# A PSUM tile of one bank for each Strassen product of the second FFN, its written-out order laid out anew, and the load of its first weights moved by one step

## The chip, the cores and the metric

The kernel runs on one core of a Trainium2 chip. The metric is the device time of one execution in microseconds, lower is better. The engines are called as the profile calls them: PE (matmul), DVE (vector), ACT (scalar), POOL, and SP, which here only issues loads. Each engine carries out its own list of instructions in order and waits at an instruction until the semaphores that it names have been reached.

## The reference

Two layers of a transformer over 512 positions with 1024 channels, in fp32. Layer 0 has a Fourier and Hyena mixer, layer 1 an attention with low-rank queries and keys (MLA); after each comes a convolutional FFN with 2816 inner columns. The change touches the second FFN and the projection ahead of it:

```python
D_MODEL = 1024
SEQ = 512
D_FF = 2816

def _dwconv3(x, w, b):
    xp = jnp.pad(x, ((0, 0), (1, 1), (0, 0)))
    return xp[:, :-2] * w[0] + xp[:, 1:-1] * w[1] + xp[:, 2:] * w[2] + b

def _conv_ffn(h, w_up, conv_w, conv_b, w_down):
    gate, val = jnp.split(h @ w_up, 2, axis=-1)
    return (jax.nn.silu(_dwconv3(gate, conv_w, conv_b)) * val) @ w_down
```

## The kernel before

Everything is kept transposed: channels on the 128 partitions, the 512 positions along the free axis. Each large product is made of three matmuls, hi·hi, hi·lo and lo·hi (`mm3`, L195 to L198), where ACT makes the rounded part hi of an operand (L171) and DVE the rest lo (L176). Weights come from HBM through the pool `W`, which has three buffers each of the raw weights `wr`, of `wh` and of `wl`; SP issues those loads in order (L184), so a load whose buffer isn't free yet holds back all loads behind it.

The output projection of the attention (`res_proj`, L1147) goes through the eight output blocks m twice, for the first 256 positions and then for the last 256. The second pass takes m in the order 5, 6, 7, (0, 1), 2, 3, 4, as j = 0 to 7, where 0 and 1 are already done. Each m adds its product to the residual stream `xr` (L1188), and the sums of squares of `xr` feed the norm whose output, hi and lo, are the tiles `hh` and `hl` that the FFN reads. `whook` is called after each m; at the step after m=3 it issues the two loads of the FFN's first weights (block 0 of `w_up`, twice 512 KB).

The second FFN (`ffn_blocks`, L1790) has 22 blocks f of 128 inner columns, each a gate half and a value half. Blocks 0 and 1 are computed whole (step `U`). Blocks 2 to 21 are computed by the Strassen-Winograd scheme, where the 1024 channels and the 512 positions are split in two: seven products P1 to P7 of 12 matmuls of 128x256, in the order P1 P2 P5 P6 P7 P4 P3, instead of eight. The additions between them:

- `S1`, `S2`, `S4` make sums of weight blocks. `S1` is POOL's four adding DMAs, `S2` (L1876) and `S4` (L1879) are DVE additions that need the block's raw weights, loaded by `Rv`. `Ha`, `La`, `Hb`, `Lb` make hi and lo of the sums, `Hv`, `Lv`, `Hg`, `Lg` those of the plain weights.
- P1, then P6 and then P4 are written to columns 0 to 255 of a PSUM tile `m`; P2 and then P7 to columns 512 to 767 of the same tile. P5 and P3 go to a tile `ms` of another tag. PSUM is 16 KB for each partition, in 8 banks of 512 fp32; `mm` tiles have 1024 columns, two banks, and there are three of them.
- `K1` (ACT, L1926) copies P1 to `t`. `C1` (DVE, L1929, fv<-t,mm) adds P2. `Ua` (t<-t,mm) adds P6, `Ub` (t<-t,mm) adds P7, `Xv` (fv<-t,ms) P5, `C2` (fg<-t,ms, L1932) and `C4` (fg<-t,mm) make the gate's two halves, `C3` (fv<-fv,ms) the value's.
- `Ca` (ACT, L1962), `Cb`, `Cc` (DVE, L1966, L1970), `Si` (ACT, L1973), `Ml` (DVE, L1976), `Ah`, `Al` are the convolution, SiLU, product with the value, and hi and lo of the result.

The blocks form groups (0 to 4, 5 to 9, 10 to 13, 14 to 17, 18 to 21). After a group its share of the product with `w_down` is made: for each of 8 output blocks a load `Rd`, `Hd` and `Ld` for hi and lo, a product `D` of 15 or 12 matmuls of 128x512 in an `mm` tile, and `X` (DVE, L2029), which adds it to `xr`. The steps D of group g stand between the P steps of later blocks.

The order of all these steps, on PE, DVE, ACT, SP and POOL, is the text `UP_ORDER` (L86): the steps are issued one by one from it, each to its engine, and nothing is reordered. A matmul that writes a tile waits for the readers of what was in it, and a reader waits for the last matmul that wrote it. Both go by the tile as a whole: the pool is opened so (`reuse_waits = "tile"`), and the tile `m` of a block is one tile, though its two halves are in different banks. What waits for what follows from the place in the list. Where C1 stands behind P6, it waits for P6, whose half it doesn't read; where it stands ahead, P6 waits for C1. P7 waits for C1 in both cases, Ua stands behind P7 and waits for it, though it reads P6, and P4 waits for Ub, though it writes where only Ua read.

Of the kernel before, what the change touches and what calls it, by code (L numbers as in the profile page):

```python
# [9 lines left out]
F32 = mybir.dt.float32  # L10
# [8 lines left out]
P = 128  # L19
# [67 lines left out]
S1.2 Rv2 Rv3 Rg2 S1.3 Hv2 S2.2 T1 Ha2 U1 Lv2 Ca0 Th1 La2 Hg2 Tl1 T3 S4.2 Th3 T2 Rv4 Hb2 Cb0 Th2 Tl3 Lb2 Tl2 S1.4 Cc0 P1.2 Ca1 T4 Si0 P2.2 Lg2 Th4 Ml0  # L87
K1.2 S2.3 P5.2 Ah0 C1.2 Hv3 Tl4 P6.2 Lv3 P7.2 Ha3 Ua2 S4.3 Xv2 P1.3 Rg3 Ub2 La3 P4.2 Rv5 K1.3 C2.2 Cb1 P3.2 S2.4 Hg3 Cc1 Lg3 P2.3 Si1 C3.2 Hb3 Ml1 P5.3
C4.2 Hv4 Lb3 Ah1 P6.3 C1.3 S1.5 Lv4 P7.3 Ha4 Ua3 S4.4 P1.4 Xv3 Rg4 Ub3 La4 P4.3 Rv6 K1.4 C2.3 Al0 P3.3 Al1 Ca2 C4.3 Hg4 Cb2 Ca3 P2.4 Lg4 Hb4 Cc2 P5.4
C3.3 Si2 Lb4 Hv5 P6.4 C1.4 S1.6 Lv5 P7.4 Ua4 S2.5 Xv4 P1.5 Ha5 Ub4 Ml2 C2.4 P4.4 Ah2 La5 K1.5 P3.4 S4.5 Cb3 Rg5 C4.4 P2.5 Cc3 Hb5 C3.4 Rv7 Al2 Si3 P5.5  # L90
Lb5 Hv6 Hg5 P6.5 C1.5 S1.7 Ca4 Lv6 P7.5 Lg5 Ua5 S2.6 P1.6 Ub5 Ha6 Xv5 C2.5 P4.5 Ml3 K1.6 La6 Ah3 P3.5 S4.6 Cb4 Rg6 P2.6 Hb6 C3.5 Cc4 S2.7 Rd0.0 P5.6
Si4 Lb6 Hv7 P6.6 Hg6 C1.6 S1.8 Lv7 P7.6 Ha7 Lg6 Ua6 C4.5 P1.7 Ub6 Xv6 C2.6 P4.6 La7 K1.7 Ml4 P3.6 S4.7 Ah4 Al3 Rg7 P2.7 Al4 Hb7 C4.6 C3.6 Rd0.1 Ca5
P5.7 Lb7 Hd0.0 Hg7 C1.7 P6.7 S1.9 Ca6 Ld0.0 Lg7 Rd0.2 P7.7 Cb5 Hd0.1 Rv8 Ua7 Cc5 D0.0 Ub7 Si5 Xv7 C2.7 Ld0.1 S2.8 Rd0.3 Ml5 P4.7 S4.8 Ah5 X0.0 Cb6 P3.7
C4.7 Cc6 D0.1 Al5 Si6 C3.7 Hd0.2 Ml6 Hv8 Ld0.2 Ca7 Lv8 Rg8 Ah6 D0.2 Cb7 Ha8 Rd0.4 X0.1 La8 Hg8 Lg8 Cc7 P1.8 Hb8 X0.2 Al6 Si7 P2.8 Lb8 K1.8 Ml7 P5.8
# [8 lines left out]
Rd1.7 Hd1.5 Ua13 Xv13 Ld1.5 D1.4 Ub13 Rv14 C2.13 S2.14 P4.13 X1.4 S4.14 P3.13 C4.13 Ca13 D1.5 Cb13 Hd1.6 C3.13 Hd1.7 Ld1.6 Ld1.7 Rv15 Cc13 Si13 D1.6
Rg14 X1.5 Hv14 Ml13 Lv14 Ah13 Hg14 S2.15 Rv16 Lg14 D1.7 Ha14 X1.6 S4.15 La14 Al13 P1.14 Hb14 X1.7 P2.14 Lb14 K1.14 S1.16 P5.14 Hv15 C1.14 P6.14 Lv15
Rg15 P7.14 Ha15 Ua14 Xv14 Rd2.0 P1.15 La15 Ub14 P4.14 C2.14 K1.15 P3.14 Hg15 C4.14 Ca14 S2.16 P2.15 Lg15 Hb15 C3.14 S4.16 P5.15 Lb15 Hv16 C1.15 P6.15
S1.17 Lv16 P7.15 Cb14 Rg16 Ha16 Ua15 Cc14 P1.16 Xv15 Rd2.1 Si14 Ub15 La16 P4.15 K1.16 C2.15 Ml14 P3.15 Hg16 C4.15 Ah14 Lg16 Ca15 P2.16 Al14 Hb16 C3.15
# [17 lines left out]
class Builder:  # L124
# [30 lines left out]
    def mm(self):  # L155
        return self.t(self.ps, [P, 1024], F32, "mm", 3)
# [62 lines left out]
    def setup(self):  # L219
# [3 lines left out]
        self.ps = self.pool("psA", space=PSUM)  # L223
        self.sm = self.pool("sm", bufs=2)
# [1532 lines left out]
    def layer1(self, x, hh, hl, steps, aw):  # L1757
# [12 lines left out]
        self.ps = self.pool("psA", space=PSUM)  # L1770
        half = [[(0, 256)], [(256, 256)]]
# [21 lines left out]
    def ffn_blocks(self, x, hh, hl, quarter, first, steps):  # L1793
# [121 lines left out]
        def P7(f):  # L1915
            prod(k_["m", f][:, 512:768], k_["wb", f], 512, tf(3))
# [24 lines left out]
        def Ub(f):  # L1941
            plus(k_["t", f][:, 2, :], k_["t", f][:, 1, :], k_["m", f][:, 512:768])
# [331 lines left out]
```

## Time and profile before

| | us |
|---|---|
| three runs | 1656.69, 1652.11, 1655.27 (median 1655.27) |
| profiled execution, whole time | 1651.85 |
| its span (first to last instruction) | 1650.0 |
| PE busy in the span | 1576.6 (96%) |
| DVE, ACT, POOL busy | 1174.0 (71%), 670.9 (41%), 166.3 (10%) |
| granted PE clock over the span | 0.988 of full |

The profiled execution is 3.42 us faster than the median of the runs and its time is 1.85 us longer than its span. The rows of the profile used below are of four kinds: waits grouped by the waiting instruction and what released it; busy time in stretches of time (windows), with the granted PE clock; single instructions in order of time (timeline), with the idle time before each in brackets and what ended it; and DMA issues with their time to landing.

### The profile page before, as it was taken

Reading aid. Unit: us, or ns where it says so; the run is one execution under the profiler, and the core shown is the slowest. Engines: PE = TensorE matmul, PEld = TensorE weight load, DVE = VectorE, ACT = ScalarE, POOL = GpSimd, SP = SyncE. Lnnn points to the kernel's source line nnn. Section 1 sums busy time; section 2 is a strip of 40 time slices with the busy share of each in tenths; the row PEclk is TensorE's granted clock in tenths of the full one; section 3 lists DMA queues with packets and bytes.
Section 4 is the critical chain, followed back from the end, with each engine's and each line's share of the span. In section 5 each row is a group of like instructions: output and inputs, shape, how many; then the busy total and the mean of one; then the engine's idle time right before and its main releaser. Section 6 shows DMA issues by size and latency. Waiting matters only on the chain. (4 is left out here: it accounts for less than half of the span.)

```text
span 1650.0 us, 22867 instructions
## 1 busy us (share of the span) xinstructions
PE 1576.6 (96%) x8968; PEld 1319.7 (80%) x8968; DVE 1174.0 (71%) x1963; ACT 670.9 (41%) x980; POOL 166.3 (10%) x245
## 2 busy tenths in 40 slices
PE   7999999999999999999999999999998899999899
PEld 5787888888888888888888877666568888888787
DVE  6779869877885356553454666899977887767784
ACT  4441234433223112221122337898855544434342
POOL 0021133000000000000000001122220121102100
PEclk9999998999999999999999999999999999999999
DMA  9336502633443245432442310000062464545433
GB/s 359 107 103 229 154 29 79 204 102 128 154 154 125 64 130 163 145 115 64 129 149 77 106 33 1 16 8 13 4 213 84 108 157 127 146 128 141 135 97 109
DMA packets 68122, 189.25 MB, mean 115 GB/s; under 512 B 7979, under 2 KB 15341, under 8 KB 66989
## 3 DMA queue, kind: packets, MB, share of 16 engines
q1 hardware_dynamic: 59053, 166.79, 31.3%
q0 software_dynamic: 8960, 20.98, 6.1%
q8 instruction: 71, 1.16, 0.3%
q14 instruction: 38, 0.31, 0.1%
HBM read 181.97 MB, written 5.77 MB: 114 GB/s over the span
## 5 line engine op out<-in xcount | busy, mean ns | idle before, releaser
L196 PE MATMUL mm<-hh,wh 128*128 128x512 f32 (+2 forms) x1192 | 395.2, 333 | 2.7 <-ACT hh L349 1.4
L197 PE MATMUL mm<-hl,wh 128*128 128x512 f32 (+2 forms) x1192 | 394.4, 331 | 2.5 <-DVE hl L358 2.3
L198 PE MATMUL mm<-hh,wl 128*128 128x512 f32 (+2 forms) x1192 | 393.2, 330 | 0.3 <-DVE wl L176 0.3
L171 ACT ACTIVATE wh<-wr 128x1024 fp32r<-128x1024 f32 (+3 forms) x187 | 177.7, 957 | 425.5 <-PE mm L197 391.5
L176 DVE TENSOR_TENSOR wl<-wr,wh 128x1024 fp32r<-128x1024 f32 (+3 forms) x187 | 207.2, 1113 | 119.7 <-ACT wh L171 119.2
L196 PEld LDWEIGHTS mm<-hh,wh 128*128 128x128 f32 x1192 | 224.7, 189 | 31.9 <-issue 2.9
L197 PEld LDWEIGHTS mm<-hl,wh 128*128 128x128 f32 x1192 | 224.5, 188 | 27.5 <-DVE hl L358 3.3
L198 PEld LDWEIGHTS mm<-hh,wl 128*128 128x128 f32 x1192 | 224.6, 188 | 22.5 <-DVE wl L176 0.9
L281 DVE SCALAR_TENSOR_TENSOR junk<-wr,sb 128x1024 bf16<-128x1024 f32 x128 | 156.2, 1221 | 50.5 <-DMA wr<-wmodT 50.5
L196 PE MATMUL mm<-ah,wh 128*128 128x512 f32 (+1 forms) x480 | 172.0, 358 | 3.8 <-ACT wh L171 3.8
L198 PE MATMUL mm<-ah,wl 128*128 128x512 f32 (+1 forms) x480 | 172.8, 360 | 2.1 <-DVE wl L176 2.1
L197 PE MATMUL mm<-al,wh 128*128 128x512 f32 (+1 forms) x480 | 171.9, 358 | 0.0
L1188 DVE SCALAR_TENSOR_TENSOR xr<-mm,mod,xr 128x512 f32<-128x512 f32 (+1 forms) x76 | 43.7, 594 | 90.6 <-PE mm L198 89.0
L196 PEld LDWEIGHTS mm<-ah,wh 128*128 128x128 f32 x480 | 90.2, 188 | 18.9 <-ACT wh L171 6.0
L198 PEld LDWEIGHTS mm<-ah,wl 128*128 128x128 f32 x480 | 90.2, 188 | 18.1 <-DVE wl L176 4.7
L197 PEld LDWEIGHTS mm<-al,wh 128*128 128x128 f32 x480 | 90.3, 188 | 13.3
L1656 PE MATMUL pv<-S,V 128*128 128x512 f32 x192 | 93.8, 597 | 2.5 <-ACT S L1635 2.5
L1610 ACT ACTIVATE S<-s,rks 128x512 f32<-128x512 f32 x96 | 62.6, 686 | 12.4 <-PE pv L1656 8.5
L411 POOL MEMSET kvh<- 128x2 f32 x1 | 0.1, 99 | 633.4 <-PE mm L197 633.4
L1656 PEld LDWEIGHTS pv<-S,V 128*128 128x128 f32 x192 | 34.4, 190 | 34.8 <-issue 29.4
L1628 POOL PARTITION_ALL_REDUCE mx<-mx x16 | 44.8, 2803 | 164.6 <-DVE mx L1625 164.6
L196 PE MATMUL mm<-th,wh 128*128 128x256 f32 x160 | 47.0, 294 | 13.7 <-DVE fv L1929 12.4
(404 smaller groups left out, 3220.4 us busy)
## 6 DMA issues: line engine op xcount, KB each, us to landing
wr<-wmodT SPq DMA_DIRECT2D x80, 512.0 KB, 3.5
wr<-w_up SPq DMA_DIRECT2D x68, 512.0 KB, 3.5
sum<-w_up POOLq DMA_DIRECT2D x80, 256.0 KB, 4.2
wm<-wmod0a SPq DMA_DIRECT2D x8, 1024.0 KB, 10.4
wr<-w_in SPq DMA_DIRECT2D x16, 512.0 KB, 3.9
wr<-w_dn SPq DMA_DIRECT2D x16, 512.0 KB, 3.5
wr<-w_out SPq DMA_DIRECT2D x13, 512.0 KB, 3.7
wr<-w_o SPq DMA_DIRECT2D x11, 512.0 KB, 3.8
```

What stands on the lines that cost most here:

```text
L171: self.nc.scalar.activation(dst, src, AF.Copy)
L176: (eng or self.nc.vector).tensor_tensor(dst, src, hi.bitcast(F32), op=ALU.subtract)
L196: mmul(out, wh, xh, start=start, stop=False)
L197: mmul(out, wh, xl, start=False, stop=False)
L198: mmul(out, wl, xh, start=False, stop=stop)
L281: nc.vector.scalar_tensor_tensor(junk, raw, 1.0, self.sb[:, j, :], op0=ALU.mult, op1=ALU.mult, accum_out=acc)
L411: self.nc.gpsimd.memset(t[:, 512:514].bitcast(F32), 0.0)
L1188: nc.vector.scalar_tensor_tensor(x[m][:, a2:b2], ps[:, a2:b2], mod[:, 8 * sec + m, c : c + 1], x[m][:, a2:b2], op0=ALU.mult, op1=ALU.add)
L1610: nc.scalar.activation(c.S[a][j // 3][:, j % 3, :], c.ps[a, j], AF.Copy, scale=c.r[:, g : g + 1])
L1628: nc.gpsimd.partition_all_reduce(c.m[a][:, 1, :], c.m[a][:, 0, :], P, bass.bass_isa.ReduceOp.max)
L1656: nc.tensor.matmul(c.P[a], V[:, j, o : o + 128], c.S[a][j // 3][:, j % 3, :], start=j == 0, stop=j == 5)
```

## The change

Three parts change, and the number of instructions on each engine stays the same.

1. In the second FFN and the projection ahead of it the `mm` tile has 512 columns, one bank, and there are six (`self.mmw`; 1024 and three elsewhere). P1, P6 and P4 of a block use one tile, P2 and P7 another of their own; blocks 0 and 1 use a tile for the gate and one for the value.
2. `UP_ORDER` is laid out anew. The sequences of PE (181 steps), SP (80 steps) and POOL (20 steps) in it stay word for word; those of DVE (436 steps) and ACT (210) change.
3. The two loads of block 0's weights are issued at the last step of the projection (j = 7) and not at the one before.

Of `UP_ORDER` the diff shows two pieces, the stretch of block 12 and that of block 3:

```diff
-Si11 Ld1.1 D1.0 Ub12 Rv13 Ml11 C2.12 Ah11 Al11 S2.13 P4.12 X1.0 S4.13 P3.12 C4.12 Ca12 D1.1 Cb12 Hd1.2 C3.12 Hd1.3 Ld1.2 Ld1.3 Rd1.4 Cc12 Rg13 Si12
+Rd1.3 D1.0 Ld1.1 Ub12 Rv13 Ml11 C2.12 Ah11 Al11 P4.12 X1.0 P3.12 S2.13 C4.12 S4.13 D1.1 Ca12 C3.12 Hd1.2 Cb12 Hd1.3 Ld1.2 Ld1.3 Rd1.4 Cc12 D1.2 Rg13
-C4.2 Hv4 Lb3 Ah1 P6.3 C1.3 S1.5 Lv4 P7.3 Ha4 Ua3 S4.4 P1.4 Xv3 Rg4 Ub3 La4 P4.3 Rv6 K1.4 C2.3 Al0 P3.3 Al1 Ca2 C4.3 Hg4 Cb2 Ca3 P2.4 Lg4 Hb4 Cc2 P5.4
+P5.3 Si1 Lb3 Hv4 P6.3 C1.3 S1.5 Lv4 P7.3 Ha4 Ua3 Rg4 Ml1 P1.4 Xv3 Ah1 Ub3 La4 Rv6 P4.3 K1.4 C2.3 Al0 P3.3 Al1 Ca2 C4.3 Hg4 Cb2 P2.4 Ca3 Lg4 Hb4 Cc2
...
     def mm(self):
-        return self.t(self.ps, [P, 1024], F32, "mm", 3)
+        return self.t(self.ps, [P, self.mmw], F32, "mm", 3072 // self.mmw)
...
+        self.mmw = 1024
...
         self.ps = self.pool("psA", space=PSUM)
+        self.mmw = 512
...
         def whook(stage, j, m):
             hook(stage, j, m)
-            if stage and j == 6:
+            if stage and j == 7:
                 first.extend(self.wload(I["w_up"][1, 0, q]) for q in range(2))
...
         def P1(f):
-            m = k_["m", f] = self.mm()
-            prod(m[:, 0:256], k_["wv", f], 0, part(0, 0))
+            k_["m", f] = self.mm()
+            prod(k_["m", f][:, 0:256], k_["wv", f], 0, part(0, 0))
 
         def P2(f):
-            prod(k_["m", f][:, 512:768], k_["wv", f], 512, part(1, 0))
+            k_["n", f] = self.mm()
+            prod(k_["n", f][:, 0:256], k_["wv", f], 512, part(1, 0))
...
         def P7(f):
-            prod(k_["m", f][:, 512:768], k_["wb", f], 512, tf(3))
+            prod(k_["n", f][:, 0:256], k_["wb", f], 512, tf(3))
...
         def C1(f):
             k_["v", f] = self.t(tm, [P, T], F32, "fv", 3)
-            plus(k_["v", f][:, 0:256], k_["t", f][:, 0, :], k_["m", f][:, 512:768])
+            plus(k_["v", f][:, 0:256], k_["t", f][:, 0, :], k_["n", f][:, 0:256])
...
         def Ub(f):
-            plus(k_["t", f][:, 2, :], k_["t", f][:, 1, :], k_["m", f][:, 512:768])
+            plus(k_["t", f][:, 2, :], k_["t", f][:, 1, :], k_["n", f][:, 0:256])
...
         def U_(f, halves, ks):
             if ("m", f) not in k_:
-                k_["m", f] = self.mm()
+                k_["m", f], k_["n", f] = self.mm(), self.mm()
```

The instructions of DVE in block 3, from the lo part of the weight sum for P7 (Lb3) to Ub3; the last number of a name is the tile's own, so equal numbers are one tile. Before:

```order
L1932 SCALAR_TENSOR_TENSOR fg_11425<-t_11335,mm_11303 128x256
L176 TENSOR_TENSOR wl_11461<-sum_11208,wh_11460 128x1024
L1929 TENSOR_TENSOR fv_11497<-t_11423,mm_11392 128x256
L176 TENSOR_TENSOR wl_11479<-wr_11284,wh_11478 128x1024
L1929 TENSOR_TENSOR t_11423<-t_11423,mm_11392 128x256
L1879 TENSOR_TENSOR sum_11297<-sum_11296,wr_11284 128x512
L1929 TENSOR_TENSOR fv_11497<-t_11423,ms_11464 128x256
L1929 TENSOR_TENSOR t_11423<-t_11423,mm_11392 128x256
```

After (the lines of the code are three further down):

```order
L176 TENSOR_TENSOR wl_11464<-sum_11209,wh_11463 128x1024
L1932 TENSOR_TENSOR fv_11498<-t_11424,mm_11446 128x256
L176 TENSOR_TENSOR wl_11484<-wr_11286,wh_11483 128x1024
L1932 TENSOR_TENSOR t_11424<-t_11424,mm_11395 128x256
L1979 TENSOR_TENSOR fq_11319<-fq_11319,mm_11223 128x512
L1932 TENSOR_TENSOR fv_11498<-t_11424,ms_11468 128x256
L1932 TENSOR_TENSOR t_11424<-t_11424,mm_11446 128x256
```

C1 (fv<-t,mm), Ua and Ub (t<-t,mm) read one tile before, 11392; now C1 and Ub read 11446, that of P2 and P7, and Ua reads 11395, that of P1 and P6. S4 of block 4 (sum) has left the stretch for an earlier place, and Ml of block 1 (L1976 before, L1979 now) has come in.

DVE where block 12 ends and the weights of block 13 are summed. Before: Al11, S2.13 (sum<-sum,wr), X1.0 (xr), S4.13 (sum), C4.12 (fg), Cb12 (fq), C3.12 (fv).

```order
L176 TENSOR_TENSOR al_12960<-fq_12853,ah_12959 128x512
L1876 TENSOR_TENSOR sum_12769<-sum_12769,wr_12954 128x512
L2029 SCALAR_TENSOR_TENSOR xr_1889_10471<-mm_12937,mod_5_74,xr_1889_10471 128x512
L1879 TENSOR_TENSOR sum_12770<-sum_12769,wr_12954 128x512
L1932 SCALAR_TENSOR_TENSOR fg_12957<-t_12828,mm_12796 128x256
L1966 SCALAR_TENSOR_TENSOR fq_12991<-fg_12957,pcol_67,fq_12991 128x511
L1929 TENSOR_TENSOR fv_12902<-fv_12902,ms_12873 128x256
```

After:

```order
L176 TENSOR_TENSOR al_12973<-fq_12878,ah_12972 128x512
L2032 SCALAR_TENSOR_TENSOR xr_1889_10471<-mm_12949,mod_5_74,xr_1889_10471 128x512
L1878 TENSOR_TENSOR sum_12781<-sum_12781,wr_12967 128x512
L1935 SCALAR_TENSOR_TENSOR fg_12970<-t_12842,mm_12808 128x256
L1881 TENSOR_TENSOR sum_12782<-sum_12781,wr_12967 128x512
L1932 TENSOR_TENSOR fv_12915<-fv_12915,ms_12886 128x256
L1969 SCALAR_TENSOR_TENSOR fq_13020<-fg_12970,pcol_67,fq_13020 128x511
```

X1.0 now stands ahead of S2.13, the instruction that waits for the load Rv13, and C4.12 ahead of S4.13.

SP's loads at the end of the projection: `w_o` of m=2, m=3 and m=4 and the first two of `w_up` are block 0's. Before:

```order
L184 DMA wr_10863<-w_o 128x1024
L184 DMA wr_10906<-w_o 128x1024
L184 DMA wr_10945<-w_up 128x1024
L184 DMA wr_10951<-w_up 128x1024
L184 DMA wr_10957<-w_o 128x1024
L184 DMA wr_11020<-w_up 128x1024
```

After:

```order
L184 DMA wr_10863<-w_o 128x1024
L184 DMA wr_10906<-w_o 128x1024
L184 DMA wr_10945<-w_o 128x1024
L184 DMA wr_10984<-w_up 128x1024
L184 DMA wr_10990<-w_up 128x1024
L184 DMA wr_11020<-w_up 128x1024
```

The load for m=4 has moved ahead of block 0's two.

More of the change, by code (lines that the diff above doesn't have):

```diff
@@ L91 @@
[L91 to L94, printed above, removed]
@@ L103 @@
[L103 to L106, printed above, removed]
@@ L1957, in gate @@
         def gate(f):
-            return k_["m", f][:, 0:512] if f < UP_WHOLE else k_["g", f]
+            return k_["m", f] if f < UP_WHOLE else k_["g", f]
         def Ca(f):
```

56 lines of the change are left out of this document (32 added, 24 removed).

## The prediction

> **What bounds the kernel now.** I read the busy times first, then PE's waits, then single stretches.
>
> ```profile
> PE 1576.6 (96%) x8968; PEld 1319.7 (80%) x8968; DVE 1174.0 (71%) x1963; ACT 670.9 (41%) x980; POOL 166.3 (10%) x245
> ```
>
> PE is the bound over the whole, so a change that leaves its 8968 matmuls as they are can only win PE's idle time. What PE waited for in the blocks of Strassen products (1290 to 1650 us; total us, times, longest):
>
> ```profile
> PE mm L196 <- DVE fv L1929: 12.4, 12, 3.4
> PE mm L196 <- DVE t L1929: 5.2, 9, 1.0
> PE mm L196 <- ACT wh L171: 5.0, 7, 1.3
> PE mm L198 <- DVE wl L176: 2.5, 6, 0.5
> ```
>
> The first two rows are 21 waits for C1 and for Ua or Ub, 17.6 us; the other two are 13 waits of D for hi and lo of its weights, 7.5 us. Each costs more than its idle time:
>
> ```profile
> 1310.08 0.28 PE L196 MATMUL mm<-th,wh 128*128 128x256 f32 x1
> 1311.69 0.42 DVE L1929 TENSOR_TENSOR fv<-t,mm 128x256 f32<-128x256 f32 x1 [1.09 <-PE mm L198]
> 1312.26 0.36 PE L196 MATMUL mm<-th,wh 128*128 128x256 f32 x1 [0.61 <-DVE fv L1929]
> 1312.45 0.28 PE L197 MATMUL mm<-quarter,wh 128*128 128x256 f32 x1
> 1312.57 0.28 PE L198 MATMUL mm<-th,wl 128*128 128x256 f32 x1
> 1313.94 0.42 DVE L1929 TENSOR_TENSOR t<-t,mm 128x256 f32<-128x256 f32 x1 [0.70 <-PE mm L198]
> ```
>
> This is block 3. Matmuls follow each other at 0.12 us, but each row lasts 0.28, so an idle time that counts from the end of a row leaves out 0.16 us: a wait costs its idle time plus 0.16. P6 starts at 1310.08; C1 waits until P6 has ended, though it reads P2's half; P7 waits for C1 and starts at 1312.26; and Ua, which needs only P6, waits for P7. The product that a step reads was long done; the wait is for the tile.
>
> **The tile of its own.** C1 now depends on P2 and K1, Ua on P6, Ub on P7; P6 waits for K1 alone, P7 for C1, P4 for Ua. In block 3 C1 comes after Lb3 while P6 runs, and P7 finds it done. So all 21 waits should go, (12.4 + 5.2) + 21 × 0.16 = 21.0 us, less two remainders.
>
> The first is the longest, 3.4 us, P6 of block 2:
>
> ```profile
> 1295.76 1.28 ACT L1973 ACT_TABLE_LOAD   x1 [1.51 <-DVE fq L1970]
> 1298.54 0.35 ACT L1926 COPY t<-mm 128x256 f32<-128x256 f32 x1
> 1299.26 1.22 DVE L176 TENSOR_TENSOR quarter<-quarter,th 128x1024 fp32r<-128x1024 f32 x1
> 1299.39 0.39 PE L196 MATMUL mm<-th,wh 128*128 128x256 f32 x1 [3.40 <-DVE fv L1929]
> ```
>
> K1 stands on ACT behind the table load for SiLU and ends at 1298.89. P6 needs it, so it can start only some 0.45 us earlier, and P7 behind it needs the lo part that DVE makes right after C1 (1299.26, 1.22 long). I take 0.3 as won here: 3.2 us of the 3.56 stay.
>
> The second is DVE's own load in blocks 2 to 6, where no D gives PE other work:
>
> ```profile
> 1300.00:1350.00 50.00, 46.25 (x382) 44.77 (x381) 43.73 (x73) 23.84 (x33) 11.58 (x16) 1.00 0.60 145
> ```
>
> 382 matmuls at 0.117 are 44.7 us of these 50. DVE (43.73 in the third column) overlaps its rows by 0.08 (in a fence below a row of 0.69 at 1450.90 is followed at 1451.51), so it occupies 43.73 − 73 × 0.08 = 37.9 us of some 45: 84%. It fits, but it does so in order, with little slack in any one block: I leave 0.8 us. The term is 21.0 − 3.2 − 0.8 = **17.0 us**; its bounds are 11 (DVE late in every second wait) and 20.6.
>
> **The waits of D.** The chain shows best where block 12 ends:
>
> ```profile
> 1450.90 0.69 DVE L1876 TENSOR_TENSOR sum<-sum,wr 128x512 f32<-128x512 f32 x1 [2.51 <-DMA wr<-w_up]
> 1451.51 0.74 DVE L2029 SCALAR_TENSOR_TENSOR xr<-mm,mod,xr 128x512 f32<-128x512 f32 x1
> 1452.17 0.68 DVE L1879 TENSOR_TENSOR sum<-sum,wr 128x512 f32<-128x512 f32 x1
> 1452.77 0.41 DVE L1932 SCALAR_TENSOR_TENSOR fg<-t,mm 128x256 f32<-128x256 f32 x1
> 1453.22 0.81 ACT L1962 ACTIVATE fq<-fg,pcol 128x512 f32<-128x512 f32 x1 [5.56 <-DVE fg L1932]
> 1453.94 1.35 ACT L171 ACTIVATE wh<-wr 128x640 fp32r<-128x640 f32 x2
> 1454.71 0.50 PE L196 MATMUL mm<-ah,wh 128*128 128x512 f32 x1 [0.63 <-ACT wh L171]
> 1455.93 0.50 PE L198 MATMUL mm<-ah,wl 128*128 128x512 f32 x1 [0.49 <-DVE wl L176]
> 1446.09 0.33 SPq L184 DMA_DIRECT2D wr<-w_up  x1
> ```
>
> S2 of block 13 idles DVE for 2.51 us for its load, issued at 1446.09 when Ld1.1 had freed a buffer. X, S4 and C4 are queued behind it; ACT's Ca waits 5.56 us for C4, Hd1.2 is queued behind Ca, and D1.2 gets its weights late. Two things change. X goes ahead of S2 and S4 behind C4: C4 starts (1451.51 − 1450.90) = 0.6 us after S2 and not 1.87, 1.26 us won. And C1 no longer holds DVE until P6 ends:
>
> ```profile
> 1442.19 0.42 DVE L1929 TENSOR_TENSOR fv<-t,mm 128x256 f32<-128x256 f32 x1 [1.74 <-PE mm L198]
> 1444.45 0.42 DVE L1929 TENSOR_TENSOR t<-t,mm 128x256 f32<-128x256 f32 x1 [0.44 <-PE mm L198]
> ```
>
> C1 goes 1.74 us earlier, Ua up to (1444.45 − 1442.19) = 2.26 earlier, the two Ld with them, and so the buffer is free and the load lands some 2 us sooner. Together that is over 3 us ahead against 0.63 + 0.49 wanted, and the other groups have the same order. The 13 waits are 7.5 + 13 × 0.16 = 9.6 us; I leave 0.6 for the first of a group, where three loads are in line: **9.0 us**, bounds 3 and 9.6. What is late next is the sums: S2 and S4 stand later in DVE's list. In block 13 La ends at 1463.24 and P5, which needs it, starts at 1465.29:
>
> ```profile
> 1462.02 1.22 DVE L176 TENSOR_TENSOR wl<-sum,wh 128x1024 fp32r<-128x1024 f32 x1
> 1465.29 0.28 PE L196 MATMUL ms<-th,wh 128*128 128x256 f32 x1
> ```
>
> That leaves 2.05 us of cover against 0.6 (one X) lost.
>
> **Block 0's weights later.** At the end of the projection PE waits for `w_o` of m=4:
>
> ```profile
> 1252.98 1.04 ACT L171 ACTIVATE wh<-wr 128x1024 fp32r<-128x1024 f32 x1
> 1256.55 1.22 DVE L176 TENSOR_TENSOR wl<-wr,wh 128x1024 fp32r<-128x1024 f32 x1
> 1258.39 0.39 PE L196 MATMUL mm<-Oh,wh 128*128 128x256 f32 x1 [2.82 <-ACT wh L171]
> 1260.42 0.58 PE L198 MATMUL mm<-Oh,wl 128*128 128x256 f32 x1 [1.53 <-DVE wl L176]
> 1264.79 0.48 DVE L1188 SCALAR_TENSOR_TENSOR xr<-mm,mod,xr 128x256 f32<-128x256 f32 x1 [2.58 <-PE mm L198]
> ```
>
> The first hi and the first lo of these rows are block 0's; the third lo in line is m=4's. In the new order m=4 takes these places: lo ends at 1257.77, its 24 matmuls at 0.12 end near 1260.5, and block 0's two lo (1.13 each) run on DVE meanwhile, until some 1261.4. The last `xr` starts there and not at 1264.79: **3.4 us**. All that follows (squares, norm, second half of block 0) hangs on that `xr`. Bounds: 0, if block 0's own weights, later by one place of 1.1 to 1.2 us on ACT and on DVE, are what PE then waits for as long; 5.7, the idle 2.82 + 1.53 and the half clock below.
>
> **The clock.** Busy PE, granted clock (third column from the end) by windows of 3.41 us:
>
> ```profile
> 1294.44:1297.85 3.41, 1.55 (x14) 1.35 (x12) 3.11 (x5) 2.08 (x3) 1.22 (x2) 1.00 0.50 118
> 1376.36:1379.77 3.41, 1.30 (x11) 1.10 (x10) 3.41 (x6) 1.70 (x4) 1.26 (x2) 1.00 0.37 141
> 1379.77:1383.18 3.41, 3.41 (x19) 3.41 (x18) 0.71 (x2) 0.74 (x1) 1.06 (x2) 0.50 0.90 185
> 1380.40 0.41 PE L197 MATMUL mm<-quarter,wh 128*128 128x256 f32 x1
> 1380.61 0.41 PE L198 MATMUL mm<-th,wl 128*128 128x256 f32 x1
> ```
>
> A window with 1.30 us of work (the wait of 2.11 us for C1 of block 8 lies in it) was followed by one at half clock: 16 matmuls at 0.21 in place of 0.117, **1.5 us** lost, which goes with the wait. The 3.40 us of block 2 were split over two windows of 1.55 and more, and no half clock followed. Some 3.1 us of that wait stay, and where they fall on the grid isn't given: in about 2.5 of the 3.41 us over which it can begin, more than 2.0 of it lie in one window, so it more likely than not costs a window at half clock, **−1.5 us**.
>
> The Trainium skill (TensorE: Matmul & The Clock Gate, Part 1: The HAM clock gate) says that half rate comes after at least one idle window of about 3.4 us, free-running. This trace agrees on length and grid, but not on idle: a window 38% busy was enough. By the page, 3.1 us could not bring a half clock, and the sum would be 1.5 us larger.
>
> **Sum.** 17.0 + 9.0 + 3.4 + 1.5 − 1.5 = 29.4 us. From the profiled execution's 1651.85 that is 1622.5; the median of the three runs is 3.4 us above that execution, so about 1626 in terms of the median.
>
> **The rivals.**
>
> *No half clock after block 2's wait.* The wait falls across two windows as it did before. For it: that is what the rows show for the same wait. Against: only some 0.9 us of 3.41 give that split. 1624.5, chance 0.12.
>
> *DVE becomes the bound where no D stands.* In blocks 2 to 7, 10 to 11, 14 to 15 and 18 to 19 PE's work per block, 84 matmuls, is 9.8 us. Half of the tile waits come back as waits for Lv, La or Lb: 17.0/2 = 8.5 lost, 1634.5. For it: ACT's table load and single-file DVE order. Against: 84%. Chance 0.13.
>
> *The loads stay late.* `wr` still has three buffers, and SP's order is unchanged, so S2 is still late; D keeps its 9.0 us: 1635. For it: 2.51 us idle before S2 is the load's. Against: the load is issued when Ld1.1 is done, which was held by C1 and Ua. Chance 0.13.
>
> *It doesn't do what it says.* If the waits still join P2's tile with P6's, only the projection's 3.4 us are won: 1652, within 0.3% of 1655.3. Chance 0.03.
>
> *The sums become the chain.* S2 and S4 stand later, and La and Lb with them; if the load of each block comes so late that P5 waits, it hits all of blocks 2 to 21. The point from which it decides: 2.05 us of cover, plus 29.4/20 = 1.5 us for each block, so S2 would have to be over 3.5 us late in every block. At 3.9, the longest wait of S2 in the trace, the loss is 20 × 1.85 = 37 us, and the time 1626 + 37 = 1663. DVE's waits for these loads:
>
> ```profile
> DVE sum L1876 <- DMA wr<-w_up: 17.6, 8, 3.9
> ```
>
> 8 of 20 wait at all, 2.2 us on average, which speaks against it. Chance 0.05.
>
> **How the numbers follow.** The forecast keeps 0.54. From the bounds of its terms, 11 + 3 + 0 at the worst and 20.6 + 9.6 + 5.7 + 1.5 at the best don't fall together; half the way to each gives its own range, 1619 to 1635. The range for 8 in 10 reaches over the two rivals near 1635: 1616 to 1638. A measurement of this kernel tells changes from about 0.3% (5 us) on. Faster: 0.54 + 0.12 + 0.13 + 0.13 = 0.92; same 0.03; slower 0.05.
>
> **What would show it.** Right: no PE wait for L1929's `fv` or `t` but one near 3 us in block 2, now released by ACT's copy; DVE's waits for PE before `fv` and `t` (C1, Ua, Ub) shorter; rows of S2 with less idle time; the last `xr` of the projection some 3 us sooner. Wrong: PE waits for `wl` or `wh` of the sums in front of P5 or P7, which would be DVE's load or the late sums; D still waiting for `wh`; or a new wait of block 0 for its weights.

## The result, and the profile after

| | before | changed |
|---|---|---|
| median of the runs taken side by side | 1655.82 us (4 runs, 1652.11 to 1656.69) | 1613.64 us (4 runs, 1611.81 to 1617.73) |
| profiled execution | 1651.85 us | 1611.81 us |
| its mean granted clock | 0.988 | 0.991 |

The ratio is 0.9753 (95% interval 0.9729 to 0.9777): the change makes the kernel faster by 2.5%, some 40 us. The forecast was 29.4 us, 1626 us with a range from 1616 to 1638; the time lies below the range. In two later comparisons of the same kernel the ratio was 0.9771 (0.9745 to 0.9796) and 0.9757 (0.9735 to 0.9779).

PE's waits from block 2 to the end of the changed kernel (total us, times, longest):

```profile
PE mm L196 <- ACT t L1929: 3.1, 1, 3.1
PE mm L198 <- DVE wl L176: 0.4, 2, 0.3
```

Before, this view had 17.6 us in 21 waits for C1, Ua and Ub and 7.5 us in 13 waits for hi or lo of weights, most of them D's. One long wait is left, P6 of block 2, now for ACT's copy K1, and two waits of D of 0.4 us together.

Block 3 in the changed kernel, the stretch that the prediction showed (the code's lines are three further down, so L1932 is what L1929 was):

```profile
1303.01 1.23 DVE L176 TENSOR_TENSOR wl<-sum,wh 128x1024 fp32r<-128x1024 f32 x1
1304.14 0.42 DVE L1932 TENSOR_TENSOR fv<-t,mm 128x256 f32<-128x256 f32 x1
1304.47 1.23 DVE L176 TENSOR_TENSOR wl<-wr,wh 128x1024 fp32r<-128x1024 f32 x1
1305.61 0.42 DVE L1932 TENSOR_TENSOR t<-t,mm 128x256 f32<-128x256 f32 x1
1305.13 0.28 PE L196 MATMUL mm<-th,wh 128*128 128x256 f32 x1
```

C1 (fv) starts at 1304.14, right behind Lb3, while P6 still runs, and P7 starts at 1305.13 with no idle time before it. Ua follows at 1305.61, without having waited for P7.

Where block 12 ends:

```profile
1425.90 0.75 DVE L2032 SCALAR_TENSOR_TENSOR xr<-mm,mod,xr 128x512 f32<-128x512 f32 x1 [0.69 <-PE mm L198]
1428.63 0.69 DVE L1878 TENSOR_TENSOR sum<-sum,wr 128x512 f32<-128x512 f32 x1 [1.98 <-DMA wr<-w_up]
1429.24 0.41 DVE L1935 SCALAR_TENSOR_TENSOR fg<-t,mm 128x256 f32<-128x256 f32 x1
1432.00 0.39 PE L196 MATMUL mm<-ah,wh 128*128 128x512 f32 x1
```

S2 still waits 1.98 us for its load, but X went ahead of it and C4 (fg) follows it at once; D1.2 starts at 1432.00 in step with the matmuls before it.

Two rows of the windows view, before and then after, from about the start of block 2 (1291.59 before, 1286.22 after) to shortly before the first D (1357.76 and 1344.99; columns: PE, PEld, DVE, ACT and POOL busy, clock, DMA share, GB/s):

```profile
1288.00:1343.00 55.00, 48.45 (x385) 46.32 (x384) 46.83 (x75) 27.67 (x37) 11.84 (x17) 1.00 0.58 140
```

```profile
1288.00:1343.00 55.00, 51.90 (x449) 51.64 (x448) 54.70 (x91) 33.00 (x46) 14.97 (x21) 1.00 0.66 161
```

In the same 55 us PE now does 449 matmuls in place of 385 (in before, 3.6 us of the window still belong to block 1), and DVE is busy for 54.70 of them. DVE has no time left there.

**Where the 40.0 us of the two profiled executions lie.** P1 of block 2 starts at 1291.59 before and at 1286.22 after, the last matmul at 1645.56 and at 1605.58. So 5.4 us are gained ahead of block 2 and 34.6 us in the stretch behind it. Of the 5.4, 2.6 lie even ahead of the projection, where the two programs do the same, as the last products of the attention show (before, then after):

```profile
1207.62 0.70 PE L1656 MATMUL pv<-S,V 128*128 128x512 f32 x1 [0.59 <-ACT S L1635]
```

```profile
1205.05 1.13 PE L1657 MATMUL pv<-S,V 128*128 128x512 f32 x2 [0.59 <-ACT S L1636]
```

Up to there the first of these executions had nine windows of 3.41 us at half clock and the second seven; at some 1.3 us each, as worked out below, two windows are about these 2.6 us, and they are chance.

The stretch can be taken apart matmul by matmul. Each one's time from its start to the next one's start, less 0.117 us for 256 columns and 0.234 for 512, is what it lost; losses over 0.12 us are called waits. The steady matmuls come out a little below 0.117, so their sum is negative.

| lost from P1 of block 2 to the end, us | before | changed | gain |
|---|---|---|---|
| waits (38 and 4) | 31.4 | 4.2 | 27.2 |
| the three matmuls behind each wait | 3.7 | 0.4 | 3.3 |
| a window at half clock | 1.5 | 0 | 1.5 |
| products (P4 aside) whose matmuls come at 118 ns or slower, over 113 ns | 4.2 | 1.7 | 2.5 |
| the rest | | | 0.1 |
| together | | | 34.6 |

### The profile page after: what moved, and what is told of

Its sections match the earlier page's. It is cut to its first block, busy times and chain, and to the rows that moved or that the text cites. A ratio compares the mean times of both kernels' runs of the same rounds, so it can differ in the third digit from the quotient of the medians.

```text
span 1610.0 us, 22860 instructions
## 1 busy us (share of the span) xinstructions
PE 1560.5 (97%) x8968; PEld 1312.2 (82%) x8968; DVE 1173.2 (73%) x1963; ACT 671.8 (42%) x980; POOL 166.3 (10%) x245
## 3 DMA queue, kind: packets, MB, share of 16 engines
q8 instruction: 70, 1.15, 0.3%
## 4 chain that ended last, share of the span: by engine, by line
PE 76%; DVE 16%; issue 2%; ACT 2%; DMA 2%; POOL 1%; SPq 0%; DVEq 0%; ACTq 0%; POOLq 0%
PE mm L196 21%; PE mm L198 21%; PE mm L197 21%; DVE wl L176 2%; PE pv L1657 2%; DVE junk L282 2%; DVE S L1633 2%; PE s L1603 1%; DVE wr L1672 1%; PE ms L196 1%; PE ms L198 1%; PE ms L197 1%; DMA wr<-w_up 1%; POOL mx L1629 1%; PE mm L662 1%
## 5 line engine op out<-in xcount | busy, mean ns | idle before, releaser
L196 PEld LDWEIGHTS mm<-hh,wh 128*128 128x128 f32 x1192 | 225.4, 189 | 31.4 <-issue 2.4
L197 PEld LDWEIGHTS mm<-al,wh 128*128 128x128 f32 x480 | 90.4, 188 | 13.6
L196 PEld LDWEIGHTS mm<-ah,wh 128*128 128x128 f32 x480 | 90.3, 188 | 13.6 <-ACT wh L171 0.5
L1657 PEld LDWEIGHTS pv<-S,V 128*128 128x128 f32 x192 | 34.5, 190 | 34.8 <-issue 29.4
L171 ACT ACTIVATE wh<-sum 128x1024 fp32r<-128x1024 f32 x40 | 42.3, 1057 | 36.4 <-PE mm L197 13.9
```

Of the source, the lines that this page charges most:

```text
L171: self.nc.scalar.activation(dst, src, AF.Copy)
L196: mmul(out, wh, xh, start=start, stop=False)
L197: mmul(out, wh, xl, start=False, stop=False)
L1657: nc.tensor.matmul(c.P[a], V[:, j, o : o + 128], c.S[a][j // 3][:, j % 3, :], start=j == 0, stop=j == 5)
```

## The experiments

All kernels were run in five rounds beside the kernel before. "Stretch" is the time from P1 of block 2 to the last matmul in the profiled execution: 354.0 us before, 319.4 in the first profile of the changed kernel and 320.9 and 319.7 in two later ones. (Before and load alone, whose programs are alike in the stretch, differ by 3.1 us in it, mostly in waits of D; a single difference of that size says little.) The last column is the sum of all losses over 0.12 us.

| kernel | ratio to before (95%) | median, us | stretch, us | PE's waits in it, us lost |
|---|---|---|---|---|
| tile alone | 0.9819 (0.9798 to 0.9839) | 1623.08 | 327.2 | 9.3 (1.5 of them matmuls at half clock) |
| order alone | 0.9926 (0.9910 to 0.9941) | 1639.95 | 341.4 | 21.0 |
| load alone | 0.9975 (0.9962 to 0.9988) | 1647.12 | 350.9 | 27.5 |
| tile and order | 0.9806 (0.9789 to 0.9822) | 1620.66 | 320.2 | 3.8 |
| changed kernel, again | 0.9771 (0.9745 to 0.9796) | 1613.20 | 320.9 | 4.8 |
| K1 early | 0.9788 (0.9766 to 0.9809) | 1617.68 | 321.7 | 4.7 |
| P4 in the other tile | 0.9790 (0.9771 to 0.9809) | 1617.89 | 322.0 | 4.5 |
| more work on DVE | 0.9848 (0.9829 to 0.9866) | 1626.76 | 332.3 | 10.6 |
| sums on POOL | 0.9843 (0.9826 to 0.9861) | 1629.39 | 331.2 | 12.7 |
| sums on POOL, K1 early | 0.9835 (0.9814 to 0.9855) | 1626.08 | 333.1 | 16.0 |
| changed kernel, a third time | 0.9757 (0.9735 to 0.9779) | 1614.39 | 319.7 | 4.8 |
| C1 late | 0.9890 (0.9864 to 0.9916) | 1636.45 | 339.1 | 22.3 |

### The parts of the change

The tile alone, with the order and the first load as before:

```diff
     def mm(self):
-        return self.t(self.ps, [P, 1024], F32, "mm", 3)
+        return self.t(self.ps, [P, self.mmw], F32, "mm", 3072 // self.mmw)
...
         def P2(f):
-            prod(k_["m", f][:, 512:768], k_["wv", f], 512, part(1, 0))
+            k_["n", f] = self.mm()
+            prod(k_["n", f][:, 0:256], k_["wv", f], 512, part(1, 0))
```

> The kernel before with the mm tile of one bank alone (P2 and P7 in a tile of their own); order of the steps and first load as before. Theory: the tile takes all the waits for C1, Ua and Ub by itself, because C1 then waits for P2, Ua for P6 and Ub for P7 wherever they stand in the list: 26 to 30 us faster than before, PE's waits for fv and t gone but for one near 3 us in block 2; waits of D get shorter too, since Ld and the load behind it are no longer held by C1, but some 3 us of them stay, because X and S4 still stand ahead of C4. Rival: the new order is what takes the waits, and the tile alone leaves DVE late at P6, P7 and P4: 12 us faster or less, with PE waiting for fv, t or wl of the sums in blocks 3 to 7.

Measured: 28.8 us between the medians (1651.83 and 1623.08). PE's waits in the stretch:

```profile
PE mm L196 <- ACT t L1929: 3.0, 1, 3.0
PE mm L196 <- ACT wh L171: 2.1, 2, 1.8
PE mm L198 <- DVE wl L176: 1.3, 4, 0.5
```

The waits for C1, Ua and Ub are gone without any new order; the rows for wh and wl are D's, 3.4 us where D had 5.9 before. The theory held, the rival fell. The tile's change also brings six tiles in place of three, but no row of PE's waits before names a last reader (fg, fq or xr) that only frees a tile for its next use, so their number had no wait to take.

The order alone, with the old tile:

```diff
-S1.2 Rv2 Rv3 Rg2 S1.3 Hv2 S2.2 T1 Ha2 U1 Lv2 Ca0 Th1 La2 Hg2 Tl1 T3 S4.2 Th3 T2 Rv4 Hb2 Cb0 Th2 Tl3 Lb2 Tl2 S1.4 Cc0 P1.2 Ca1 T4 Si0 P2.2 Lg2 Th4 Ml0
+S1.2 Rv2 Rv3 Rg2 S1.3 Hv2 S2.2 T1 Hg2 U1 Ha2 Lv2 Th1 La2 Ca0 Tl1 T3 S4.2 Th3 T2 Rv4 Hb2 Cb0 Th2 Tl3 Lb2 Tl2 S1.4 Cc0 P1.2 T4 Ca1 Si0 P2.2 Lg2 Th4 Ml0
...
```

> The kernel before with the new order of the steps alone; mm tile of two banks and first load as before. Theory: the waits for C1, Ua and Ub stay (20 us or more of PE's idle time), only the waits of D get shorter: 1 to 6 us faster than before. Rival (the order takes the waits): 15 us faster or more.

Measured: 11.9 us, between the two. PE's waits:

```profile
PE mm L196 <- DVE fv L1929: 10.1, 12, 3.6
PE mm L196 <- DVE t L1929: 4.6, 7, 1.1
PE mm L196 <- ACT wh L171: 1.2, 2, 0.6
PE mm L198 <- DVE wl L176: 0.3, 1, 0.3
```

The waits for the tile stay, 14.7 us in 19, though the theory had 20 us or more. The waits of D go altogether (none of the rows left is a D: matmul by matmul, all 27 waits are of P products), which I had put at the order and the tile together. Each of the two takes part of D's waits by itself, so their gains don't add up: 28.8 and 11.9 alone, and together:

```diff
-            if stage and j == 7:
+            if stage and j == 6:
```

> The changed kernel with the two loads of block 0's weights at their old place. Theory: the parts add up, so it is 3 to 5 us slower than the changed kernel, 36 to 39 us faster than before. Rival: the load's place matters only with the old order: within 1 us of the changed kernel.

Measured for tile and order without the load's move (the changed kernel with the line above): 31.2 us between the medians, ratio 0.9806, where the whole change gave 0.9753 to 0.9771. By these the load's move is worth 5.8 to 8.8 us, with some 5 us of uncertainty, over what either theory said. For the load alone:

```diff
-            if stage and j == 6:
+            if stage and j == 7:
```

> The kernel before with the two loads of block 0's weights one step later alone. Theory: m=4 of the projection no longer waits for its weights (idle 2.8 and 1.5 us before), the last xr comes 3.4 us sooner and all behind it: 3 to 5 us faster than before. Rival: block 0's own weights are then what PE waits for, as long: 0 to 1 us faster.

Measured: ratio 0.9975, 4.1 us (2 to 6), in the theory's band. But m=4 still waits: 2.0 us for its lo, where before it waited 2.8 and 1.5. The two measures of the load's move differ mostly by the granted clock, the subject of the next runs: the five runs of tile and order all had a mean clock of 0.985 or 0.986, those of the changed kernel 0.986 to 0.992, and the three at 0.986 took 1617.7 to 1619.1 us beside 1618.0 to 1621.5. In the profiles, the time from the first matmul of the projection to P1 of block 2 is 69.6 us before and 68.8 with the load alone, 73.7 in tile and order with three windows at half clock, and 66.8 to 68.3 in the changed kernel with one or two.

### The scatter of the runs: windows at half clock

> The changed kernel once more, beside three of its variants on one chip. Theory: half-clock windows of PE are a matter of where each execution falls on their grid, and they make up the scatter of the runs; the first runs of the changed kernel had about 10 of them and the median of before more, so the ratio comes out a little smaller here: 33 to 40 us faster than before. Rival: the scatter has another cause, and times don't go with the mean granted clock.

> The changed kernel beside the two others, as their reference: 1611 to 1616 us in the median, with its runs spread over some 8 us along with the mean granted clock.

Measured: 37.7 us and 40.8 us between the medians; the changed kernel's runs spread from 1610.35 to 1619.10. Over its 13 runs in three comparisons, those with a mean clock of 0.991 or 0.992 took 1611.5 us in the mean, those at 0.986 1618.4. Time goes with the clock that was lost, one minus the mean clock times the span, at 0.74 us for each us (correlation 0.92); in 44 runs of before the slope is 0.75 (correlation 0.67). A window of 3.41 us at half clock is 1.7 us of clock, so it costs some 1.3 us. The same wait, P6 of block 2, in the first profile and in the second of the changed kernel (PE busy is the first column behind the length):

```profile
1288.79:1292.20 3.41, 1.67 (x15) 1.48 (x14) 3.25 (x4) 1.88 (x3) 1.48 (x2) 1.00 0.53 120
1292.20:1295.60 3.40, 2.04 (x17) 2.04 (x18) 3.26 (x5) 3.22 (x6) 0.86 (x1) 1.00 0.84 165
```

```profile
1290.32:1293.74 3.42, 0.92 (x8) 0.72 (x7) 3.12 (x5) 2.72 (x3) 1.38 (x2) 1.00 0.69 155
1293.74:1297.15 3.41, 2.96 (x14) 2.96 (x15) 3.13 (x4) 2.08 (x5) 0.08 (x1) 0.50 0.83 157
```

In the first the wait falls across two windows, neither under 1.67 us of work, and the clock stays; in the second one window holds 0.92 us of work, and the next one runs at half clock. So the same program, with the same wait, pays or doesn't by where its window grid lies. The theory held, as far as the slopes and this pair of profiles show it.

### What is left: P6 of block 2, and DVE

K1 ahead of SiLU's table load in block 2, C1 and Lv3 ahead of T4:

```diff
-S1.2 Rv2 Rv3 Rg2 S1.3 Hv2 S2.2 T1 Hg2 U1 Ha2 Lv2 Th1 La2 Ca0 Tl1 T3 S4.2 Th3 T2 Rv4 Hb2 Cb0 Th2 Tl3 Lb2 Tl2 S1.4 Cc0 P1.2 T4 Ca1 Si0 P2.2 Lg2 Th4 Ml0
-K1.2 S2.3 P5.2 Ah0 C1.2 Hv3 Tl4 P6.2 Lv3 P7.2 Ha3 Ua2 S4.3 Xv2 P1.3 Rg3 Ub2 La3 P4.2 K1.3 Rv5 C2.2 Cb1 P3.2 S2.4 Cc1 C4.2 P2.3 Hg3 C3.2 Hb3 S4.4 Lg3
+S1.2 Rv2 Rv3 Rg2 S1.3 Hv2 S2.2 T1 Hg2 U1 Ha2 Lv2 Th1 La2 Ca0 Tl1 T3 S4.2 Th3 T2 Rv4 Hb2 Cb0 Th2 Tl3 Lb2 Tl2 S1.4 Cc0 P1.2 Ca1 P2.2 K1.2 Hv3 C1.2 P5.2 Si0 Lv3 T4 P6.2 Ua2 Th4 P7.2 Lg2 P1.3
+Tl4 Xv2 Rg3 Ub2 C2.2 S2.3 P4.2 Ha3 Ml0 Ah0 La3 S4.3 K1.3 Rv5 Cb1 P3.2 S2.4 Cc1 C4.2 P2.3 Hg3 C3.2 Hb3 S4.4 Lg3
```

> The changed kernel with a new order for the stretch of block 2 alone: K1 ahead of the table load for SiLU on ACT, C1 and the lo part of block 3's weights ahead of T4 on DVE. Theory: the wait of 3.1 us of P6 in block 2 was for K1 behind that load; it falls to under 1 us (P4 then waits a little for the lo part of T4), no half clock follows it, and the kernel is 2 to 4 us faster than the changed kernel. Rival: P6, P7 or P1 of block 3 then wait as long for something else on DVE, which is busy all through this stretch: within 1 us.

Measured: 1617.68 us beside 1613.20, and 321.7 beside 320.9 us in the stretch: no gain. P6 of block 2 no longer waits, but P7 of block 3 does, for C1:

```profile
PE mm L196 <- DVE fv L1932: 3.1, 1, 3.1
PE mm L198 <- DVE wl L176: 0.6, 1, 0.6
PE mm L197 <- DVE quarter L176: 0.3, 1, 0.3
```

The rival held, one block later than it said (its "within 1 us" fits the stretch and not the medians): the 3 us are DVE's work between the norm and block 3, and moving one step of it moves the wait.

Three more additions on DVE in each block:

```diff
         def Xv(f):
+            for _ in range(3):
+                plus(k_["t", f][:, 0, :], k_["t", f][:, 1, :], k_["t", f][:, 1, :])
             plus(k_["v", f][:, 256:512], k_["t", f][:, 1, :], k_["b", f][:, 0:256])
```

> The changed kernel with three more additions of 128x256 on DVE in each of the 20 Strassen blocks, right ahead of Xv: some 1.0 us of DVE work per block, which is not used. Theory: DVE was loaded to about 84% in blocks 2 to 7 and less elsewhere, so 20 us of work cost PE 2 to 8 us, most of it in blocks 3 to 7. Rival (DVE was at its limit there, and the forecast's remainder of 0.8 us was luck): each added us is lost where no D stands, 10 us or more.

Measured: 13.6 us slower in the medians than the changed kernel on the same chip, 11.4 in the stretch. The rival held: more than half of the 20 us of added work is lost. Not only where no D stands, as it said: matmul by matmul, D's waits rose to 3.6 us (0.9 to 1.4 in the changed kernel), 3.3 us of waits of P3 are new, and products at 118 ns and slower lose 4.7 us (0.7 to 1.7 in the changed kernel).

The sums of blocks 3 to 7 on POOL:

```diff
-            v.tensor_tensor(s[:, 0:512], s[:, 512:1024], k_["rv", f][:, 0:512], op=ALU.add)
+            (nc.gpsimd if 3 <= f <= 7 else v).tensor_tensor(s[:, 0:512], s[:, 512:1024], k_["rv", f][:, 0:512], op=ALU.add)
...
-            v.tensor_tensor(k_["sb", f][:, 0:512], k_["sa", f][:, 0:512], k_["rv", f][:, 512:1024], op=ALU.add)
+            (nc.gpsimd if 3 <= f <= 7 else v).tensor_tensor(k_["sb", f][:, 0:512], k_["sa", f][:, 0:512], k_["rv", f][:, 512:1024], op=ALU.add)
```

> The changed kernel with the sums S2 and S4 of blocks 3 to 7 on POOL in place of DVE (10 additions of 128x512, 0.69 us each on DVE; the like took 1.3 to 1.9 us on POOL in other places of the trace); the order is kept. Theory: DVE works without a gap from block 2 to block 7, but PE no longer waits for it after block 2, and P6 of block 2 waits for K1 on ACT, so nothing is won: within 2 us of the changed kernel. Rival: the 5 us taken from DVE come back as shorter time: 3 us faster or more; or POOL is so slow that PE waits for the sums: 3 us slower or more.

> Both: the new stretch of block 2 with K1 ahead of the table load, and the sums of blocks 3 to 7 on POOL. Theory: in the first of the two alone the wait of 3.1 us came back one block later, P7 of block 3 for C1, because DVE had no time to spare; with 2.4 us of sums off DVE ahead of that C1, that wait falls to under 1.5 us: 1 to 4 us faster than the changed kernel. Rival: the additions on POOL slow DVE down or come late themselves, and the wait stays at 2.5 us or more.

Measured: 15.0 us slower than the changed kernel alone, 11.7 with K1 early. POOL's instructions and DVE's longest wait, of the first of the two, in blocks 2 to 6:

```profile
L1874 POOL DMA_DIRECT2D sum<-w_up x8 | 7.2, 897 | 9.1 <-DMA sum<-w_up 9.1
L1878 POOL TENSOR_TENSOR sum<-sum,wr 128x512 f32<-128x512 f32 x4 | 6.8, 1690 | 7.6 <-issue 7.6
```

```profile
DVE wl L176 <- ACT wh L171: 13.9, 5, 3.7
```

An addition of S2 takes 1.69 us on POOL (0.69 on DVE), and it stands in line behind POOL's own adding DMAs, which wait 9.1 us for the copies that they add to. The sums come late, so does their hi part on ACT, and DVE waits 13.9 us for it. DVE's load did fall (40.52 us busy of the 55 where the changed kernel had 54.70), and the sums became the chain. With K1 early as well, the wait of P7 of block 3 did fall, to 0.25 us idle, as the theory said, but P5 of block 3 waits 4.89 us for the hi part of its sum. So POOL came too late, the last of the rivals in both expectations.

### P4's wait alone

```diff
         def P4(f):
-            prod(k_["m", f][:, 0:256], k_["wg", f], 0, tf(4))
+            prod(k_["n", f][:, 0:256], k_["wg", f], 0, tf(4))
```

with C4 reading the same tile.

> The changed kernel with P4 written to the tile of P2 and P7, so that P4 waits for Ub again as it did before; nothing else. Theory: a wait for a tile's last reader costs PE in itself, whatever the order: 10 or more waits for t come back, 5 to 9 us slower than the changed kernel, each wait costing its idle time plus about 0.25 us (0.16 that the idle time leaves out, and a slow second matmul). Rival: the new order has made Ub early enough that P4 hardly waits: within 2 us of the changed kernel.

Measured: a single wait for Ub came back (0.4 us idle, block 18), so the theory of ten waits fell. The median is 4.7 us over the changed kernel's, which the stretch does not show (322.0 against 320.9 us); its runs have clocks of 0.984 to 0.988. With the old tile P4 did wait for Ub (part of the 4.6 us for t in the run of the order alone); that this came from C1 and Ua being held there is suggested by the two runs and not shown by itself.

### The price of a wait

C1 behind Ua in blocks 3 to 20, so that P7 waits for P6's reader again:

```diff
-P5.3 Si1 Lb3 Hv4 P6.3 C1.3 S1.5 Lv4 P7.3 Ha4 Ua3 Rg4 Ml1 P1.4 Xv3 Ah1 Ub3 La4 Rv6 P4.3 K1.4 C2.3 Al0 P3.3 Al1 Ca2 C4.3 Hg4 Cb2 P2.4 Ca3 Lg4 Hb4 Cc2
+P5.3 Si1 Lb3 Hv4 P6.3 S1.5 Lv4 Ua3 C1.3 P7.3 Ha4 Rg4 Ml1 P1.4 Xv3 Ah1 Ub3 La4 Rv6 P4.3 K1.4 C2.3 Al0 P3.3 Al1 Ca2 C4.3 Hg4 Cb2 P2.4 Ca3 Lg4 Hb4 Cc2
...
```

> The changed kernel with one kind of wait put back in blocks 3 to 20: Ua (which waits for P6) stands ahead of C1 on DVE, and both ahead of P7, so that P7 waits for C1 behind P6 as it did before; the tiles stay apart. Theory of the price of a wait: up to 18 waits of P7 of some 0.6 to 0.9 us idle; from P1 of block 2 to the end PE loses for each its idle time, plus 0.16 that the idle time leaves out, plus about 0.15 to 0.2 in slower matmuls behind it (the term that the forecast left out): 1.0 to 1.2 us each, 16 to 22 us in all. Rival (what the forecast used): idle time plus 0.16 alone, 0.8 to 1.0 each, with the matmuls behind a wait as fast as elsewhere. Third: DVE, with no time to spare in blocks 3 to 7, makes its own waits on top, at P4 and P3.

Measured: 18 waits, and nothing else new (the code's lines are one further up in this kernel).

```profile
PE mm L195 <- DVE fv L1931: 16.2, 18, 0.9
PE mm L195 <- ACT t L1928: 3.1, 1, 3.1
```

One of them, with the matmuls around it (every third row, the hi·hi products):

```profile
1412.40 0.28 PE L195 MATMUL mm<-th,wh 128*128 128x256 f32 x1
...
1412.74 0.28 PE L195 MATMUL mm<-th,wh 128*128 128x256 f32 x1
...
1414.77 0.39 PE L195 MATMUL mm<-th,wh 128*128 128x256 f32 x1 [0.84 <-DVE fv L1931]
...
1415.22 0.28 PE L195 MATMUL mm<-th,wh 128*128 128x256 f32 x1
...
1415.58 0.28 PE L195 MATMUL mm<-th,wh 128*128 128x256 f32 x1
...
1415.93 0.28 PE L195 MATMUL mm<-th,wh 128*128 128x256 f32 x1
```

Start to start the 18 waits lost 19.1 us: 0.90 idle and 0.16 each, as the forecast had it. But the three matmuls behind the wait take 0.45 (1414.77 to 1415.22), those after them 0.36 and 0.35, those before it 0.34. Over the 18 waits the first of these effects makes 1.7 us more than the same matmuls take in the changed kernel, 0.10 each; the second comes behind 12 of the 18 and ends at a later product.

The whole stretch is 18.2 to 19.7 us longer than in the three profiles of the changed kernel, which had 0 to 1.4 us of half clock in it where this one has none; with that taken out it is 19.6 to 20.8, or 1.09 to 1.15 for each wait. With the idle time as it came out, the rival's rule gives 1.06, and the theory's, with 0.15 to 0.2 more, 1.21 to 1.26. So the added term is there, but it is the 0.10 of the matmuls right behind the wait; the slower products behind it don't show in the sum (2.1 us in this kernel, 0.7 to 1.7 in the changed one). That the total lies in the theory's band of 16 to 22 us doesn't decide between the two. The third theory fell.

## Why the prediction was too small

**The waits for the tile: the mechanism right, the split wrong.** The forecast had 17.0 us for them and 9.0 for D; the waits lost 27.2 us less. The tile takes its part without the new order, as shown by the tile alone. But not all of the 13 waits for hi or lo were D's:

```profile
1549.75 0.50 PE L196 MATMUL mm<-ah,wh 128*128 128x512 f32 x1 [1.26 <-ACT wh L171]
1556.82 0.38 PE L198 MATMUL mm<-hh,wl 128*128 128x256 f32 x1 [0.34 <-DVE wl L176]
1586.66 0.36 PE L196 MATMUL mm<-th,wh 128*128 128x256 f32 x1 [0.60 <-ACT wh L171]
```

The first is a D (it reads ah), the second P1 of block 18 and the third P7 of block 20; P7 of block 16 is another. They went with the tile alone. Counted by product, the P steps won 20.4 us and D 6.8; that 17.0 and 9.0 come near in their sum is in part luck.

**The price of a wait: the step that failed.** "A wait costs its idle time plus 0.16" leaves out that the matmuls right behind it are slow. In before the three matmuls behind each of 38 waits lost 3.7 us, in the changed kernel 0.4: 3.3 us that no term of the forecast had. With 18 waits put back by themselves (C1 late) it was 0.10 us a wait, and the forecast's 34 waits at 0.10 are 3.4 us. The row that shows it was quoted in the prediction (1312.26 to 1312.45, 0.19 us) and not used. A further 2.5 us lie in products that run at 118 ns a matmul or slower in place of 113. These can't be put down to the waits: C1 late, with 19 waits, loses 2.1 us in such products, and the kernel with more work on DVE, with 16 losses over 0.12 us, 4.7. Their cause stays open. Together these two are 5.8 us of the 10.6 us that lie between the forecast of 29.4 and the 40.0 of the profiled executions. The others are the waits (1.2), the clock (1.5), the part ahead of block 2 (2.0, since 2.6 lay ahead of the change) and the rest of the table (0.1).

The bounds could not have caught it: all the best ends together are 37.4 us, some 1618 us in terms of the median, which is still above the 1613.64 measured. (Half the way to each end also gives 1622 to 1634, and not the 1619 to 1635 that the prediction states.)

**The clock: a coin, counted as a rule.** The forecast set the half window lost before (1.5 us) against a new one behind block 2's wait. In the first profile none came: that is the rival with chance 0.12, but it isn't the program that decides. Of the twelve traces in which this wait is, a half window followed it in nine, about the share that was worked out. What the forecast had no term for is the clock outside these two places: its mean rose from 0.986 (44 runs) to 0.989 (13 runs), 23 against 18 us of clock lost, some 4 us of time. That fewer long waits leave fewer such windows fits this, but where the windows lay in runs without a trace isn't known.

**The projection: 2.8 us of the 3.4 forecast.** (That is from its first matmul to P1 of block 2; in two later profiles, with one more window at half clock each, it is 2.1 and 1.3.) The order of events was right: the last `xr` follows the two lo parts of block 0's weights on DVE. The rows of the changed kernel:

```profile
1257.11 1.22 DVE L176 TENSOR_TENSOR wl<-wr,wh 128x1024 fp32r<-128x1024 f32 x1
1258.59 1.22 DVE L176 TENSOR_TENSOR wl<-wr,wh 128x1024 fp32r<-128x1024 f32 x1
1259.72 0.48 DVE L1189 SCALAR_TENSOR_TENSOR xr<-mm,mod,xr 128x256 f32<-128x256 f32 x1
```

**DVE's slack: wrong in the working, harmless in the sum.** The 43.73 us busy of 50 are already the time in which at least one row ran; the overlap of the rows was taken off a second time. DVE was loaded to 98% of what PE would need (43.73 against 44.7), not to 84%. After the change it is busy 54.70 of 55 us, and PE lost nothing by it; what the slack would have hidden is shown by the added work, more than half of which was lost. DVE as the bound was one of the rivals; it is now a bound beside PE, and no step of the prediction had noticed that the change arrives just at it.

**P6 of block 2: the size right, the reason wrong.** 3.2 us were to stay and 3.26 did, released by ACT's copy, as forecast. But the lo part at 1299.26 belongs to P4 and not to P7, and moving K1 ahead doesn't help: the limit is DVE's queue.

**The waits of D: 9.0 forecast, 6.8 won of the 7.7 that there were.** With X and C4 ahead, the order alone takes them all. The tile alone takes 2.5 of their 5.9 us idle. That this goes by the link that the forecast named, from C1 to Ld to the load to S2, isn't shown: S2's waits for its loads were 17.6 us before, 18.9 with the tile alone and 8.6 with the order alone, so their shortening goes with the order, in which S2 stands later, and not with the tile.

**The step from the profiled execution to the median** added 3.4 us, because the three runs shown had a median that much above it. Over 48 runs the median of before is 1653.1, 1.3 above the profiled execution, so most of the step was chance. With 1.8 us by which the changed kernel's median lies above its own profile, 10.6 + 3.4 − 1.8 makes the 12 us between 1626 and 1613.64.

The rivals in short: the waits did go by the tile and not by the bank of each half, so the change did what it says; S2's waits for its loads fell to 11.4 us, and the sums never held up P5:

```profile
DVE sum L1878 <- DMA wr<-w_up: 11.4, 7, 2.4
```

## What to carry to other kernels

A tile that spans two banks ties together the readers and writers of both halves where the waits go by tiles; a tile for each product took such waits away here with the old order and with the new. When the idle time of a busy engine is summed up as a gain, take the rows behind each wait too: here the slow restart was an eighth on top of what the waits lost (3.3 of 27.2 us). And read the load of the engine beside it before expecting more: once PE's waits were gone, DVE was at 99% in the same stretch, and every further step that only moved work moved the wait along.

## What the runs showed of the hardware

Matmuls of 128x256 come at one of two rates, 113 or 118 ns apart in the mean of a product: over the 14 traces 1069 and 551 of 1662 products, P4's left out, which come at 118 to 120 ns nearly everywhere. A stream keeps its rate from product to product: in 1106 pairs of neighbours with no wait, half window, D or P4 between them, none changed it. In the run with C1 late, 12 of 18 waits were followed by the slow rate and 6 by the fast one. What decides it wasn't tried.

The half clock doesn't need an idle window. Over the 14 traces, from the projection on, all 27 full-speed windows of 3.41 us in which PE was busy for 0.14 to 0.42 of the time were followed by one at half clock, from 0.45 to 0.48 two of four, from 0.49 to 0.54 none of six, and at 0.55 to 0.58 six of seventeen, all six in the short waits of block 0. The Trainium skill (TensorE: Matmul & The Clock Gate, Part 1: The HAM clock gate) asks for an idle window; a window that was 0.42 busy was enough here. To leave the half clock took more: all ten windows at half clock that were 0.23 to 0.83 busy were followed by a second one, and none of the 35 that were 0.87 busy or more.
